# The last block's last three output tiles in two halves of 256 tokens, in a written order, with weights and residuals held in free buffers

## The chip, the cores and the metric

The kernel runs on one core of one Trainium2 chip. The metric is the device time of one execution in microseconds. The core has TensorE (PE in the rows, its weight loads PEld), VectorE (DVE), ScalarE (ACT), GpSimd (POOL), and DMA engines that are fed by the queues of SyncE (SP) and of ACT.

## What is computed

Two layers of a bidirectional encoder trunk over 2048 tokens of 1024 channels, then a final RMSNorm. What matters here is the end of the second layer:

```python
    gate = jax.nn.sigmoid(gate_lg + gate_b).reshape(bsz, seq, N_BRANCH, D_MODEL)
    y = gate[:, :, 0] * y_a + gate[:, :, 1] * y_b
    return y @ w_out
...
        x = x + hybrid_mixer(h, w_in[l], qkv_conv_w[l], a_log[l], dt_bias[l], dn_norm_w[l],
...
    return rms_norm(x, final_norm_w)
```

The product with `w_out` and the residual give x for all 1024 channels of a token; only then is the token's mean square known, and each channel is scaled by its inverse root and by `final_norm_w`.

## The kernel before

Channels lie on the 128 partitions, tokens along the free axis. `merge` of the last layer works on halves of 1024 tokens: for each it makes the gated sum y, split into a high and a low part (`yhi`, `ylo`), and calls `last_out`. `last_out` runs over two blocks of 512 tokens. In a block, j runs over eight output tiles of 128 channels. For each j, `dense` issues 24 matmuls of 512 columns (8 steps over the input channels, three each: high weight by high y, L174, high weight by low y, L175, low weight by high y, L176) into a PSUM bank `pd`; DVE adds the residual `xr` (L1304) into `xl`; ACT squares it (L225) and DVE adds the square to `ss` (L226). After the eighth tile, `token_sum` (L200) sums the squares over the partitions with matmuls of one column, `rsqrt` makes the inverse root with nine short DVE operations, `spread` makes a diagonal `dg` (L206) and spreads it over the partitions with matmuls of 128 columns (L208), and eight DVE operations of 512 columns (L1317) scale the tiles, each followed by the store of its tile (L1320), even j on SP's queue and odd j on ACT's.

The weights of a tile come through `weight`: two transfers of 256 KB each into one of two buffers `wraw`, then a split in ACT (L157, high part `whi`) and in DVE (L158, low part `wlo`). A transfer into a `wraw` buffer waits until DVE has split what lay in it two transfers earlier. `whi` and `wlo` have two buffers each, so weights are made ready one tile ahead. The tiles `xr`, `sq` and `dg` share three buffers. Large buffers come from a pool of four; in the last half two of them hold the gate products' operands (`uop`, `gop`), which nothing reads after the gates of that half, and two hold `yhi` and `ylo`.

Nothing in `last_out` has an order written out: a scheduler places each instruction on its engine's queue, by its estimates of when the operands are there, and within an engine the queue is run in order. SP's queue holds the loads of weights and residuals and half of the stores in one row, so a load that waits holds back all that stand behind it. `bind(start)` fixes the order as written for all instructions issued since `mark()`, on PE, ACT, DVE and POOL; SP is left out of it.

Of the kernel before, what the change touches and what calls it, by code (L numbers as in the profile page):

```python
# [14 lines left out]
P = 128  # L15
L = 2048
HALF = 1024
NB = 512
D = 1024
KD = 8  # L20
# [4 lines left out]
EPS = 1e-6  # L25
# [5 lines left out]
STEP = (4, 4, 4, 4)  # L31
TAIL = (3, 3, 2)
Z = '121'
LATE = 4
AHEAD = 4
R2 = 3.7
# [40 lines left out]
class Trunk:  # L77
# [79 lines left out]
        self.nc.scalar.activation(hi, src, AF.Copy)  # L157
        self.nc.vector.tensor_tensor(out=lo, in0=src, in1=hi.bitcast(F32), op=ALU.subtract)  # L158

    def weight(self, src, kk):  # L160
        hi = self.pw.tile([P, KD, P], F32R, tag="whi", bufs=2, name="whi")[:, 0:kk, :]
        lo = self.pw.tile([P, KD, P], F32R, tag="wlo", bufs=2, name="wlo")[:, 0:kk, :]
# [35 lines left out]
    def token_sum(self, ps, src, n):  # L198
        for i in range(n):
            self.nc.tensor.matmul(ps[:, i:i + 1], src[:, i * P:(i + 1) * P], self.ones[:, 0:1],  # L200
                                  start=True, stop=True)

    def spread(self, ps, r, n):
        dg = self.pst.tile([P, NB], F32, tag="st", name="dg").rearrange("p (a b) -> p a b", b=P)
        for i in range(n):
            self.nc.vector.tensor_scalar(out=dg[:, i, :], in0=self.ident, scalar1=r[:, i:i + 1],  # L206
                                         scalar2=None, op0=ALU.mult)
            self.nc.tensor.matmul(ps[:, i * P:(i + 1) * P], self.ones, dg[:, i, :], start=True, stop=True)  # L208
# [11 lines left out]
    def add_square(self, ss, x, first):  # L220
        if first:
            self.nc.scalar.activation(ss, x, AF.Square)
        else:
            sq = self.st("sq")
# [518 lines left out]
    def conformer_norm(self, blk):  # L743
# [12 lines left out]
        yield 1.8  # L756
        for _ in range(int(Z[0])):
            yield 0.0
# [8 lines left out]
        yield 4.0  # L767
        for _ in range(int(Z[1])):
            yield 0.0
# [6 lines left out]
        yield 1.5  # L776
        for _ in range(int(Z[2])):
            yield 0.0
# [502 lines left out]
    def late_norm(self, xn, ss, wcol):  # L1281
        for _ in range(LATE):
            yield
        r = self.norm_stats(ss)
        yield
        yield
        yield from self.normalise(1, xn, r, wcol)

    def last_out(self, l, half, xd, fnw, yhi, ylo, ahead):
        nc, a = self.nc, self.a  # L1290
        v_ = nc.vector
        for b in range(2):
            sl = slice(b * NB, (b + 1) * NB)
            tk = slice(half * HALF + b * NB, half * HALF + (b + 1) * NB)
            xn = [t[:, i * NB:(i + 1) * NB] for t in (self.mid("xl"), self.mid("xl")) for i in range(4)]
            ss = self.hm("ss")[:, 0:NB]
            w = self.weight(a["w_out"][l, 0], KD)
            for j in range(KD):
                next(ahead, None)
                ps = self.pd()  # L1300
                self.dense(ps, w, lambda k: (yhi[:, k, sl], ylo[:, k, sl]), KD)
                xr = self.st("xr")
                self.load(xr, xd[j][:, tk])
                v_.tensor_tensor(out=cut(xn[j]), in0=sort(ps), in1=cut(xr), op=ALU.add)  # L1304
                self.add_square(ss, xn[j], j == 0)
                if j + 1 < KD:
                    w = self.weight(a["w_out"][l, j + 1], KD)
            ps = self.pz()
            self.token_sum(ps, ss, 4)
            v = self.sm(4, "nv")  # L1310
            r = self.sm(4, "nr")
            v_.tensor_scalar(out=v, in0=ps[:, 0:4], scalar1=1.0 / D, scalar2=EPS, op0=ALU.mult, op1=ALU.add)
            self.rsqrt(r, v, 4)
            pr = self.pz()
            self.spread(pr, r, 4)
            for j in range(KD):
                v_.scalar_tensor_tensor(out=xn[j], in0=xn[j], scalar=fnw[:, j:j + 1], in1=pr,  # L1317
                                        op0=ALU.mult, op1=ALU.mult)
                eng = nc.scalar if j % 2 else nc.sync
                eng.dma_start(a["out"][j, :, tk], xn[j])  # L1320


def layout(inputs, depth):
# [49 lines left out]
```

## Time and profile before

| | |
|---|---|
| median of 3 runs | 3189.29 us (3188.14 to 3192.9) |
| the profiled execution | 3187.47 us |
| its span | 3185.7 us |
| PE busy | 3090.6 us, 97% of the span |
| DVE busy | 2398.4 us, 75% |
| ACT busy | 1385.3 us, 43% |
| mean granted TensorE clock | 0.993 |

The profiled execution is 1.77 us longer than its span and 1.82 us shorter than the median. Times of rows are counted from the start of the span. A busy share over the whole span says little of the last 60 us, in which everything that is changed lies; there the timeline, the chain of work that ended last and the busy time of stretches are read. The granted clock of 1.00 is TensorE's 2.4 GHz, 0.50 its 1.2 GHz.

### The profile page before, as it was taken

The page shows a single profiled execution, that of the slowest core. Times are in us where ns is not written, and L with a number is a line of the kernel's source. Part 1 is how long each engine was busy: PE and PEld are TensorE (multiplying, and loading weights), DVE is VectorE, ACT ScalarE, POOL GpSimd, SP SyncE. Part 2 cuts the span into 40 slices and gives each one's busy share as a digit, 9 for nine tenths or more (in the row PEclk, how much of TensorE's full clock was granted, in tenths as well). Part 3 has the DMA queues.
Part 4 walks back from the last instruction along what each step waited for, and adds up shares of the span by engine and source line. Part 5 has one row for each costly group of instructions (what it writes and reads, how often), then busy time and mean ns, then how long its engine had stood idle before and what let it go on. Part 6 is the DMA issues. An engine that isn't in the chain of part 4 may idle for free. (4 is left out here: it accounts for less than half of the span.)

```text
span 3185.7 us, 51259 instructions
## 1 busy us (share of the span) xinstructions
PE 3090.6 (97%) x19110; PEld 2705.8 (85%) x19110; DVE 2398.4 (75%) x4409; ACT 1385.3 (43%) x3104; POOL 302.3 (9%) x297
## 2 busy tenths in 40 slices
PE   6999999999999999999999999999999999999997
PEld 5788888888889998787888888888888999878786
DVE  7789898987646697745676989898955567867655
ACT  5625151522444466533345242425234445655332
POOL 3000000000122231000000000000002222200000
PEclk9999999999999999999999999999999999999999
DMA  4323222334687886654413131414357777855634
GB/s 141 90 96 93 87 93 87 93 112 133 206 288 247 258 267 208 198 185 133 135 53 101 66 120 60 120 60 123 117 186 261 243 252 255 283 182 192 204 126 146
DMA packets 427545, 501.70 MB, mean 157 GB/s; under 512 B 96224, under 2 KB 260704, under 8 KB 427296
## 3 DMA queue, kind: packets, MB, share of 16 engines
q1 hardware_dynamic: 354544, 388.58, 39.2%
q10 hardware_dynamic: 64688, 80.09, 7.3%
q0 software_dynamic: 8064, 29.76, 2.5%
q8 instruction: 150, 2.46, 0.3%
q14 instruction: 99, 0.81, 0.1%
HBM read 342.74 MB, written 155.58 MB: 156 GB/s over the span
## 5 line engine op out<-in xcount | busy, mean ns | idle before, releaser
L174 PE MATMUL pd<-h,whi 128*128 128x512 f32 x2816 | 1092.1, 388 | 0.0
L176 PE MATMUL pd<-h,wlo 128*128 128x512 f32 x2816 | 1070.4, 380 | 1.9 <-DVE wlo L158 1.9
L175 PE MATMUL pd<-h,whi 128*128 128x512 f32 x2816 | 1070.9, 380 | 0.0
L728 DVE SCALAR_TENSOR_TENSOR cacc<-gp,vec,cacc 128x1009 f32<-128x1009 f32 (+1 forms) x480 | 614.3, 1280 | 37.5 <-ACT cacc L726 34.3
L176 PEld LDWEIGHTS pd<-h,wlo 128*128 128x128 f32 x2816 | 533.8, 190 | 79.3 <-DVE wlo L158 3.5
L174 PEld LDWEIGHTS pd<-h,whi 128*128 128x128 f32 x2816 | 534.0, 190 | 79.0 <-issue 1.4
L175 PEld LDWEIGHTS pd<-h,whi 128*128 128x128 f32 x2816 | 534.5, 190 | 72.4 <-issue 1.9
L157 ACT ACTIVATE whi<-wraw 128x512 fp32r<-128x512 f32 x400 | 242.7, 623 | 473.2 <-PE pd L175 335.9
L158 DVE TENSOR_TENSOR wlo<-wraw,whi 128x512 fp32r<-128x512 f32 x400 | 275.0, 701 | 142.1 <-ACT whi L157 141.8
L553 DVE SCALAR_TENSOR_TENSOR acc<-cin,vec,acc 128x1022 f32<-128x1022 f32 (+1 forms) x192 | 246.5, 1299 | 14.4 <-ACT acc L551 13.2
L176 PE MATMUL pd<-yhi,wlo 128*128 128x512 f32 x512 | 194.9, 381 | 3.8 <-DVE wlo L158 3.7
L174 PE MATMUL pd<-yhi,whi 128*128 128x512 f32 x512 | 194.6, 380 | 0.9 <-ACT whi L157 0.9
L175 PE MATMUL pd<-ylo,whi 128*128 128x512 f32 x512 | 194.0, 379 | 0.0
L808 ACT ACTIVATE go<-pd,vec 128x512 f32<-128x512 f32 x128 | 87.1, 680 | 147.9 <-PE pd L176 138.2
L529 ACT ACTIVATE cin<-pd 128x512 f32<-128x512 f32 x96 | 57.0, 594 | 154.7 <-PE pd L176 154.6
L176 PEld LDWEIGHTS pd<-yhi,wlo 128*128 128x128 f32 x512 | 96.8, 189 | 19.9 <-DVE wlo L158 6.4
L740 ACT ACTIVATE ao<-pd 128x512 f32<-128x512 f32 x64 | 38.3, 598 | 170.0 <-PE pd L176 169.9
L174 PEld LDWEIGHTS pd<-yhi,whi 128*128 128x128 f32 x512 | 96.8, 189 | 15.4 <-ACT whi L157 2.0
L175 PEld LDWEIGHTS pd<-ylo,whi 128*128 128x128 f32 x512 | 96.8, 189 | 13.6
L174 PE MATMUL pd<-uop,whi 128*128 128x512 f32 x256 | 101.0, 395 | 6.6 <-ACT whi L157 6.5
L176 PE MATMUL pd<-uop,wlo 128*128 128x512 f32 x256 | 99.1, 387 | 2.3 <-DVE wlo L158 1.4
L175 PE MATMUL pd<-gop,whi 128*128 128x512 f32 x256 | 97.7, 381 | 3.0 <-DVE gop L158 3.0
(297 smaller groups left out, 4754.9 us busy)
## 6 DMA issues: line engine op xcount, KB each, us to landing
wraw<-w_in SPq DMA_DIRECT2D x240, 256.0 KB, 3.3
gt<-go ACTq DMA_DIRECT2D x128, 256.0 KB, 3.6
dl<-gr SPq DMA_DIRECT2D x128, 256.0 KB, 5.2
dl<-kq SPq DMA_DIRECT2D x64, 512.0 KB, 6.1
dl<-kv SPq DMA_DIRECT2D x64, 512.0 KB, 5.8
wraw<-w_out SPq DMA_DIRECT2D x96, 256.0 KB, 3.0
kq<-acc SPq DMA_DIRECT2D x16, 1024.0 KB, 5.5
gr<-go ACTq DMA_DIRECT2D x64, 256.0 KB, 2.2
```

The source lines that it names most:

```text
L157: self.nc.scalar.activation(hi, src, AF.Copy)
L158: self.nc.vector.tensor_tensor(out=lo, in0=src, in1=hi.bitcast(F32), op=ALU.subtract)
L174: mm(ps, whi[:, k, :], xhi, start=k == 0, stop=False)
L175: mm(ps, whi[:, k, :], xlo, start=False, stop=False)
L176: mm(ps, wlo[:, k, :], xhi, start=False, stop=k == kk - 1)
L529: nc.scalar.activation(cut(t[:, o + b * NB:o + (b + 1) * NB]), sort(ps), AF.Copy)
L553: self.nc.vector.scalar_tensor_tensor(out=out, in0=t[:, k:k + n], scalar=wc(k), in1=out, op0=ALU.mult, op1=ALU.add)
L728: self.nc.vector.scalar_tensor_tensor(out=acc, in0=t[:, k:k + n], scalar=wc(k), in1=acc, op0=ALU.mult, op1=ALU.add)
L740: nc.scalar.activation(cut(o), sort(ps), func)
L808: nc.scalar.activation(cut(o), sort(ps), AF.Identity, bias=self.vec[:, V_GB + j:V_GB + j + 1])
```

## The change

For the last block of the last half, the first five tiles (`PART`) run as before. The weights of tiles 5, 6 and 7 are loaded during tiles 1, 2 and 3 into a free large buffer (`wend`), through the same two `wraw` buffers, and their residuals into another (`xend`). Then the three tiles run first for tokens 0 to 255 of the block and then for tokens 256 to 511, as matmuls of 256 columns, in an order fixed by `bind`. The closing steps (token sum, root, spread, scaling, stores) run once for each half: those of the first half stand among the products of the second. The square of the last tile of a half isn't added to `ss`; a second group of one-column matmuls adds it in PSUM (`token_add`). The lines of `after` are numbered higher, as L146 for the load that was L145, L158 and L159 for the split, L178 to L180 for the three matmuls, L209 and L217 for the sum and the spread, L1307 for the residual's addition, L1331 for the scaling.

```diff
-    def weight(self, src, kk):
+    def weight(self, src, kk, kept=None):
+        if kept:
+            hi, lo = kept
...
+    def token_add(self, ps, src, n, first, last):
+        for i in range(n):
+            self.nc.tensor.matmul(ps[:, i:i + 1], src[:, i * P:(i + 1) * P], self.ones[:, 0:1],
+                                  start=first and i == 0, stop=last, skip_group_check=True)
...
+        def close(o, n, sq):
+            q = n // P
+            c = slice(o % NB, o % NB + n)
+            ps = self.pz()
+            self.token_add(ps, ss[:, c], q, True, sq is None)
+            if sq is not None:
+                self.token_add(ps, sq, q, False, True)
...
+            self.rsqrt(r, v, q)
+            yield
+            pr = self.pz()[:, 0:n]
+            self.spread(pr, r, q)
+            yield
+            for j in range(KD):
+                x = xn[j][:, c]
+                v_.scalar_tensor_tensor(out=x, in0=x, scalar=fnw[:, j:j + 1], in1=pr, op0=ALU.mult, op1=ALU.mult)
+                eng = nc.scalar if j % 2 else nc.sync
+                eng.dma_start(a["out"][j, :, half * HALF + o:half * HALF + o + n], x)
+                yield
...
+            whole = PART if half and b else KD
+            if whole < KD:
+                hold = self.big([P, 2, KD, NB], F32R, "wend").rearrange("p a b c -> p (a b c)")
+                parts = [hold[:, i * D:(i + 1) * D].rearrange("p (k c) -> p k c", c=P) for i in range(2 * (KD - whole))]
+                ws = []
+                spare = self.big([P, 8192], F32, "xend")
+                late = [spare[:, i * NB:(i + 1) * NB] for i in range(KD - whole)]
...
+                if j + 1 < whole:
                     w = self.weight(a["w_out"][l, j + 1], KD)
...
+                if whole < KD and j and len(ws) < KD - whole:
+                    i = len(ws)
+                    ws.append(self.weight(a["w_out"][l, whole + i], KD, parts[2 * i:2 * i + 2]))
+                    self.load(late[i], xd[whole + i][:, half * HALF + o:half * HALF + o + NB])
...
+            start = self.mark()
+            n = NB // 2
+            first = iter(())
+            for h in range(2):
+                g = o + h * n
+                for i, (j, w) in enumerate(zip(range(whole, KD), ws)):
+                    p = product(j, w, g, n, late[i][:, h * n:h * n + n])
+                    if h and i == 1:
+                        run(first, 1)
+                    if h and i == 2:
+                        run(p, 3)
+                        run(first, 1)
+                        run(p, 5)
+                        run(first, 4)
+                    run(p)
+                    x = xn[j][:, h * n:h * n + n]
+                    if j + 1 < KD:
+                        self.add_square(ss[:, h * n:h * n + n], x, False)
+                sq = self.st("sq")[:, 0:n]
+                nc.scalar.activation(sq, x, AF.Square)
+                c = close(g, n, sq)
+                if h == 0:
+                    first = c
+                else:
+                    run(first, 2)
+                    run(c, 1)
+                    run(first)
+                    run(c)
+            self.bind(start)
```

Up to the third tile of the last block (j = 2) the order on every engine is the same as before. Three places differ in what the prediction needs. The first is SP's queue from the residual of j = 2 on. Before, the weights of j = 3 stand there (`wraw_27828`, `wraw_27832`), then those of j = 4 (`wraw_27869`, `wraw_27873`) and of j = 5:

```order
L145 DMA xr_27820<-x1_11761 128x512
L145 DMA wraw_27828<-w_out 128x512
L145 DMA wraw_27832<-w_out 128x512
L145 DMA wraw_27869<-w_out 128x512
L145 DMA wraw_27873<-w_out 128x512
L145 DMA xr_27861<-x1_11761 128x512
L145 DMA wraw_27910<-w_out 128x512
L145 DMA wraw_27914<-w_out 128x512
```

Now `wraw_27797` and `wraw_27801` are the weights of j = 5, which are kept, `wraw_27839` and `wraw_27843` those of j = 3, `wraw_27847` and `wraw_27851` those of j = 6, `wraw_27889` and `wraw_27893` those of j = 4:

```order
L146 DMA xr_27806<-x1_11761 128x512
L146 DMA wraw_27797<-w_out 128x512
L146 DMA wraw_27801<-w_out 128x512
L146 DMA xend_27706<-x1_11761 128x512 x2
L146 DMA wraw_27839<-w_out 128x512
L146 DMA wraw_27843<-w_out 128x512
L146 DMA xr_27856<-x1_11761 128x512
L146 DMA xend_27706<-x1_11761 128x512
L146 DMA wraw_27847<-w_out 128x512
L146 DMA wraw_27851<-w_out 128x512
L146 DMA wraw_27889<-w_out 128x512
L146 DMA wraw_27893<-w_out 128x512
```

So two transfers of kept weights and two residuals stand ahead of the weights of j = 3, and two more with a third residual ahead of those of j = 4.

The second place is ACT around the square of j = 3. Before, the square (`sq_27864`) stands behind the splits for j = 4 (`whi_27867`) and j = 5 (`whi_27908`):

```order
L157 ACTIVATE whi_27867<-wraw_27869 128x512
L157 ACTIVATE whi_27867<-wraw_27873 128x512
L157 ACTIVATE whi_27908<-wraw_27910 128x512
L157 ACTIVATE whi_27908<-wraw_27914 128x512
L225 ACTIVATE sq_27864<-xl_27702 128x512
```

Now the square of j = 3 (`sq_27884`) stands ahead of the split for j = 4 (`whi_27887`), behind that for j = 6:

```order
L158 ACTIVATE wend_27705<-wraw_27847 128x512
L158 ACTIVATE wend_27705<-wraw_27851 128x512
L234 ACTIVATE sq_27884<-xl_27702 128x512
L158 ACTIVATE whi_27887<-wraw_27889 128x512
L158 ACTIVATE whi_27887<-wraw_27893 128x512
```

The split for j = 4 has moved behind an operation that needs the product of j = 3.

The third place is the end of DVE's queue. Before, the root (its last step is L196) is followed by the diagonal and eight scalings of 512 columns:

```order
L195 TENSOR_TENSOR rst_28039<-rst_28039,nr_28037 128x4
L196 SCALAR_TENSOR_TENSOR nr_28037<-rst_28039,nr_28037 128x4
L206 TENSOR_SCALAR dg_28053<-con_90,nr_28037 128x128 x4
L1317 SCALAR_TENSOR_TENSOR xl_27702<-xl_27702,fnw_96,pz_28052 128x512 x4
L1317 SCALAR_TENSOR_TENSOR xl_27703<-xl_27703,fnw_96,pz_28052 128x512 x4
```

Now, behind the second half's root, the last two scalings of the first half (with `pz_28112`) come first:

```order
L200 SCALAR_TENSOR_TENSOR nr_28154<-rst_28156,nr_28154 128x2
L1331 SCALAR_TENSOR_TENSOR xl_27703<-xl_27703,fnw_96,pz_28112 128x256 x2
L215 TENSOR_SCALAR dg_28174<-con_90,nr_28154 128x128 x2
L1331 SCALAR_TENSOR_TENSOR xl_27702<-xl_27702,fnw_96,pz_28173 128x256 x4
L1331 SCALAR_TENSOR_TENSOR xl_27703<-xl_27703,fnw_96,pz_28173 128x256 x4
```

So ten scalings of 256 columns stand behind the last root instead of eight of 512. On PE, the first half's token sum stands behind the first product of the second half, and its spread behind nine matmuls of that half's third product.

## Rows read from the trace of the kernel before

**Rows 1.** The timeline (start, length, engine, line, operation, count), PE alone, from the last matmul of the last product on.

```profile
3166.97 0.38 PE L176 MATMUL pd<-yhi,wlo 128*128 128x512 f32 x1
3169.58 1.55 PE L200 MATMUL pz<-con,ss 128*128 128x1 f32 x8 [2.22 <-DVE ss L226]
3173.74 2.08 PE L208 MATMUL pz<-dg,con 128*128 128x128 f32 x8 [2.62 <-DVE dg L206]
```

**Rows 2.** The timeline, DVE alone, over the last two products and the closing steps.

```profile
3162.21 0.69 DVE L1304 TENSOR_TENSOR xl<-pd,xr 128x512 f32<-128x512 f32 x1 [1.43 <-PE pd L176]
...
3167.39 0.69 DVE L1304 TENSOR_TENSOR xl<-pd,xr 128x512 f32<-128x512 f32 x1 [3.04 <-PE pd L176]
3168.83 0.69 DVE L226 TENSOR_TENSOR ss<-ss,sq 128x512 f32<-128x512 f32 x1 [0.74 <-ACT sq L225]
3171.16 0.16 DVE L1312 TENSOR_SCALAR nv<-pz 128x4 f32<-128x4 f32 x1 [1.64 <-PE pz L200]
...
3173.40 0.87 DVE L206 TENSOR_SCALAR dg<-con,nr 128x128 f32<-128x128 f32 x4
3175.86 5.36 DVE L1317 SCALAR_TENSOR_TENSOR xl<-xl,fnw,pz 128x512 f32<-128x512 f32 x8 [1.58 <-PE pz L208]
```

**Rows 3.** The chain of work that ended last, in order of time (start, length, what), from the weights of j = 3 to the first low-part matmul of j = 4.

```profile
3135.03 4.15 DMA wraw<-w_out
...
3139.28 0.64 ACT whi L157
...
3139.95 0.70 DVE wlo L158
3140.66 4.62 DMA wraw<-w_out
...
3145.39 0.64 ACT whi L157
3146.07 0.48 PE pd L174
...
3146.80 0.48 PE pd L176
```

**Rows 4.** The timeline, PE alone: the first low-part matmul of j = 2, its last matmul and the first of j = 3.

```profile
3135.05 0.48 PE L176 MATMUL pd<-yhi,wlo 128*128 128x512 f32 x1 [1.42 <-DVE wlo L158]
...
3139.69 0.38 PE L176 MATMUL pd<-yhi,wlo 128*128 128x512 f32 x1
3139.97 0.48 PE L174 MATMUL pd<-yhi,whi 128*128 128x512 f32 x1
```

**Rows 5.** The tile `wraw` from 3120 us on: time from the issue of a transfer to its landing.

```profile
DMA to landing us min/median/max: 2.4/2.9/4.7
```

**Rows 6.** The timeline, PE alone: the previous block's token sum (eight one-column matmuls), the first matmul behind it, and that block's spread.

```profile
3122.97 1.05 PE L200 MATMUL pz<-con,ss 128*128 128x1 f32 x8
3123.89 0.46 PE L174 MATMUL pd<-yhi,whi 128*128 128x512 f32 x1
...
3126.65 1.16 PE L208 MATMUL pz<-dg,con 128*128 128x128 f32 x8
```

**Rows 7.** The timeline, PE alone, in the delta rule's stage: sixteen matmuls of 128 columns and what follows them.

```profile
1241.44 1.95 PE L983 MATMUL pz<-dl,dl 128*128 128x128 f32 x16
1243.32 0.23 PE L924 MATMUL pz<-dh,dh 32*32 32x32 f32 x4
```

**Rows 8.** Groups of weight loads by line and form (count, busy us, mean ns of one, idle time before).

```profile
L176 PEld LDWEIGHTS pd<-yhi,wlo 128*128 128x128 f32 x512 | 96.8, 189 | 19.9 <-DVE wlo L158 6.4
...
L983 PEld LDWEIGHTS pz<-dl,dl 128*128 128x128 f32 x512 | 62.2, 192 | 1.7
```

**Rows 9.** The same view of DVE: operations of 128, 512 and 256 columns.

```profile
L972 DVE SCALAR_TENSOR_TENSOR dl<-pz,neg,dl 128x128 f32<-128x128 f32 x240 | 66.4, 343 | 17.8 <-PE pz L967 17.1
...
L1317 DVE SCALAR_TENSOR_TENSOR xl<-xl,fnw,pz 128x512 f32<-128x512 f32 x32 | 21.4, 743 | 3.0 <-PE pz L208 2.9
...
L694 DVE TENSOR_TENSOR sol<-sol,solt 128x256 f32<-128x256 f32 x8 | 3.4, 421 | 0.2
```

**Rows 10.** The same view of ACT: operations of 128 and 512 columns.

```profile
L976 ACT ACTIVATE dm<-pz,eg 128x128 f32<-128x128 f32 x240 | 68.6, 368 | 56.6 <-PE pz L970 56.6
...
L225 ACT ACTIVATE sq<-xl 128x512 f32<-128x512 f32 x28 | 17.4, 622 | 13.1 <-DVE xl L1304 9.8 <-issue 3.0 <-DMA gt<-gt 0.2
```

**Rows 11.** Busy time of each engine in stretches (length, then PE, PEld, DVE, ACT, POOL busy with counts, then granted clock, DMA share, GB/s): around two idle times of PE earlier in the program.

```profile
1230.70:1234.60 3.90, 0.00 (x0) 0.00 (x0) 1.77 (x3) 3.87 (x9) 0.00 (x0) 1.00 0.56 192
1234.60:1238.00 3.40, 3.08 (x14) 3.08 (x15) 3.35 (x10) 0.44 (x2) 1.26 (x1) 0.50 0.73 218
1238.00:1241.00 3.00, 3.00 (x46) 2.58 (x45) 2.86 (x11) 2.35 (x7) 1.25 (x1) 1.00 0.84 223
...
1447.80:1449.90 2.10, 0.06 (x1) 0.00 (x0) 0.52 (x1) 2.10 (x4) 0.00 (x0) 1.00 0.00 0
1449.90:1453.00 3.10, 2.96 (x13) 2.29 (x13) 2.58 (x5) 0.98 (x2) 0.00 (x0) 1.00 0.52 75
```

**Rows 12.** The same view of the end: the last four products, and what comes behind them.

```profile
3146.00:3167.40 21.40, 21.25 (x96) 17.98 (x96) 10.53 (x17) 6.57 (x12) 0.00 (x0) 1.00 0.38 123
3167.40:3185.70 18.30, 3.62 (x16) 3.24 (x16) 9.47 (x26) 0.63 (x1) 0.00 (x0) 0.57 0.31 115
```

More of the change, by code (lines that the diff above doesn't have):

```diff
@@ L33 @@
 Z = '121'
+PART = 5
 LATE = 4
@@ L158, in split @@
         self.nc.vector.tensor_tensor(out=lo, in0=src, in1=hi.bitcast(F32), op=ALU.subtract)
-    def weight(self, src, kk):
-        hi = self.pw.tile([P, KD, P], F32R, tag="whi", bufs=2, name="whi")[:, 0:kk, :]
-        lo = self.pw.tile([P, KD, P], F32R, tag="wlo", bufs=2, name="wlo")[:, 0:kk, :]
+    def weight(self, src, kk, kept=None):
+        if kept:
+            hi, lo = kept
+        else:
+            hi = self.pw.tile([P, KD, P], F32R, tag="whi", bufs=2, name="whi")[:, 0:kk, :]
+            lo = self.pw.tile([P, KD, P], F32R, tag="wlo", bufs=2, name="wlo")[:, 0:kk, :]
         for k in range(0, kk, 4):
@@ L223, in add_square @@
         else:
-            sq = self.st("sq")
+            sq = self.st("sq")[:, 0:x.shape[1]]
             self.nc.scalar.activation(sq, x, AF.Square)
@@ L1291, in last_out, with product, residual @@
         v_ = nc.vector
+        def product(j, w, o, n, xr):
+            sl = slice(o, o + n)
+            ps = self.pd()[:, 0:n]
+            yield from self.dense_steps(ps, w, lambda k: (yhi[:, k, sl], ylo[:, k, sl]), KD)
+            x = xn[j][:, o % NB:o % NB + n]
+            v_.tensor_tensor(out=cut(x), in0=sort(ps), in1=cut(xr), op=ALU.add)
+        def residual(j, o, n):
+            xr = self.st("xr")[:, 0:n]
+            self.load(xr, xd[j][:, half * HALF + o:half * HALF + o + n])
+            return xr
@@ new lines, in close @@
+        def close(o, n, sq):
[5 more added lines that the diff above has]
+                self.token_add(ps, sq, q, False, True)
+            v = self.sm(q, "nv")
+            r = self.sm(q, "nr")
+            v_.tensor_scalar(out=v, in0=ps[:, 0:q], scalar1=1.0 / D, scalar2=EPS, op0=ALU.mult, op1=ALU.add)
+            self.rsqrt(r, v, q)
[9 more added lines that the diff above has]
+                yield
@@ L1292, in last_out, with run @@
+        def run(g, n=1000):
+            for _ in range(n):
+                if next(g, self) is self:
+                    return
         for b in range(2):
-            sl = slice(b * NB, (b + 1) * NB)
-            tk = slice(half * HALF + b * NB, half * HALF + (b + 1) * NB)
+            o = b * NB
             xn = [t[:, i * NB:(i + 1) * NB] for t in (self.mid("xl"), self.mid("xl")) for i in range(4)]
             ss = self.hm("ss")[:, 0:NB]
+            whole = PART if half and b else KD
[5 more added lines that the diff above has]
+                late = [spare[:, i * NB:(i + 1) * NB] for i in range(KD - whole)]
@@ L1297, in last_out @@
             w = self.weight(a["w_out"][l, 0], KD)
-            for j in range(KD):
+            for j in range(whole):
                 next(ahead, None)
[L1300 to L1304, printed above, removed]
+                run(product(j, w, o, NB, residual(j, o, NB)))
+                if self.rate:
+                    self.follow()
@@ L1305, in last_out @@
                 self.add_square(ss, xn[j], j == 0)
-                if j + 1 < KD:
+                if j + 1 < whole:
                     w = self.weight(a["w_out"][l, j + 1], KD)
[L1308 to L1320, printed above, removed]
+                if whole < KD and j and len(ws) < KD - whole:
+                    i = len(ws)
+                    ws.append(self.weight(a["w_out"][l, whole + i], KD, parts[2 * i:2 * i + 2]))
+                    self.load(late[i], xd[whole + i][:, half * HALF + o:half * HALF + o + NB])
@@ new lines, in last_out @@
+            if whole == KD:
+                run(close(o, NB, None))
+                continue
+            start = self.mark()
[21 more added lines that the diff above has]
+                    first = c
+                else:
+                    run(first, 2)
+                    run(c, 1)
+                    run(first)
+                    run(c)
```

## The prediction

> **What bounds the kernel now.** I read the stretches first: in the last four products PE is busy 21.25 of 21.40 us, behind them 3.62 of 18.30 us, and DVE 9.47 [rows 12]. So PE bounds the program up to its last product, and behind it a chain. The timelines of PE and DVE show the chain [rows 1, 2]: the last matmul is issued at 3166.97, DVE takes its bank at 3167.39 (0.42 later), then residual, square, `ss`, token sum, root from 3171.16, diagonal at 3173.40, spread, eight scalings from 3175.86 to 3181.22, stores, end at 3185.7. That is 18.3 us in which nothing overlaps. Half of the tokens could go through these steps under the other half's products, which is the part that the change takes up.
>
> The third view is the chain of waits ahead of it [rows 3]. The two transfers of j = 3 are issued at 3135.03, the first takes 4.15 us, its split 0.64 in ACT and 0.70 in DVE, and only then, at 3140.66, does a buffer come free for j = 4's first: a turn of 5.63 us, while a product takes 5.18 (3162.21 to 3167.39 [rows 2]). The stretch is supplied barely in time: j = 3 starts 0.28 us after the last matmul of j = 2 is issued (3139.69, 3139.97 [rows 4]), j = 4 waits for its weights [rows 3]. The change puts more loads into just this stretch.
>
> **Supply: j = 3.** In SP's queue the kept weights of j = 5 now stand where those of j = 3 stood; both pass through the same two `wraw` buffers, so j = 3's weights get the turn that j = 4 had, issued at 3140.66 [rows 3]. Their landing takes 2.4 to 4.7 us [rows 5]; the same turn took 4.62 with a residual behind it [rows 3]; I take 3.4, between the median of 2.9 and that. With 0.11 to the start of ACT, 0.64 of split and 0.04, PE starts j = 3 at 3144.8 instead of 3139.97 (3143.8 at 2.4, 3146.1 at 4.62). Nothing else stands ahead in PE's queue, so the 4.8 us are idle.
>
> **Supply: j = 4.** Call the start of j = 3 S. Two bounds follow. By the loads: the split of j = 3's first piece ends at S + 0.7, then come j = 6's first piece (2.9 + 0.1 + 0.64 + 0.70) and j = 4's (2.9 + 0.1 + 0.64 + 0.05): S + 8.7. By ACT's order: the square of j = 3 now stands ahead of the split of j = 4's weights, so that product has to end first. Its first low-part matmul comes 0.73 after its first (as at 3146.07 and 3146.80 [rows 3]) instead of 0.43, so S + 0.3 + 5.18 + 0.2 for the product to reach DVE, 0.69 for the residual, 0.1, 0.64 for the square, 0.64 for the split: S + 7.8. I take S + 8.7. Then j = 4 lasts 5.18 and 0.35 more for three matmuls of tile 5 that the scheduler put between its first and its third, which cover the wait for the low part. PE is past j = 4 at S + 14.2.
>
> **The narrow products.** 72 matmuls of 512 columns (0.216 each, 5.18 / 24) become 144 of 256. The trace has none of 256 in this form. From below: half of 0.216 is 0.108. From above: 0.216, as if width didn't matter. The nearest rows are those that the weight load paces: eight one-column matmuls in 0.92 us, 0.115 each [rows 6], sixteen of 128 columns in 1.88, 0.118 each [rows 7], and the loads last alike in both kinds, 189 and 192 ns [rows 8]. I take 0.115: 141 behind j = 4 make 16.2 us.
>
> The Trainium skill ("TensorE: Matmul & The Clock Gate", "The mechanism") says that a weight load overlaps a running matmul only where the two use other row groups. Here all 128 rows are used, so by it each load would stand beside its matmul. The rows speak against it: 0.216 for 512 columns at 2.4 GHz is 0.213 of streaming, so loads of 128 columns are hidden there. What it would give is the second rival.
>
> **Work put between the products.** The first half's token sum, eight passes, 0.9 [rows 6]; its spread, four of the eight passes of [rows 6], 0.45; and a wait ahead of that spread: DVE makes the diagonal behind tile 6's residual, square and `ss` (0.2 + 0.42 + 0.5 + 0.42 + 0.3), while only nine matmuls (1.0) stand between: 0.8. The last matmul then reaches DVE 0.2 us after the pace. So DVE gets the last bank at S + 14.2 + 16.2 + 0.9 + 0.45 + 0.8 + 0.2 = S + 32.75 = 3177.55, instead of 3167.39: **10.2 us later**. Of these, 4.8 come ahead of S, 3.5 from the wait for j = 4 (8.7 - 5.18), 1.0 from the narrow matmuls (16.55 for 15.5) and 2.2 from the closing steps, less 1.5 of waits that the old stretch held (3139.97 to 3167.39 is 27.4 us, five products are 25.9).
>
> **The end.** A DVE operation of 256 columns lasts 0.42 [rows 9] against 0.69 [rows 2]. ACT's square, between 0.368 at 128 and 0.622 at 512 columns [rows 10], is 0.45. Scaling: 743 - 343 ns for 384 columns [rows 9] makes 0.476 for 256, and in a row 0.40 each (5.36 for eight of 512 is 0.66 each). The chain: residual 0.42, square 0.45, no `ss`, two hand-overs 0.1, four passes of the sum 0.6 (1.05 for eight at full clock [rows 6]), root 2.24 as before (3171.16 to 3173.40 [rows 2]), two scalings of the first half that stand ahead of the diagonal 0.8, diagonal to PE 0.35, four passes of the spread 0.9 (half of 1.16 [rows 6] to half of 2.08 [rows 1], the clock being 0.57 there [rows 12]), eight scalings 3.3, and 4.48 from the last scaling to the end as before (3181.22 to 3185.7). Sum 13.65 against 18.3: **4.65 us less**. The first half's scalings and stores lie under tile 7's last matmuls; without that cover they would add 3.3.
>
> **Sum.** 10.2 - 4.65 = +5.5 us on the profiled execution's 3187.47: 3193.0. The median lies 1.82 above that execution, so 3189.29 + 5.5 = **3194.8 us**. A measurement of this kernel tells 0.2%, 6.4 us, from no change; the forecast is just inside. Bounds of the case: with landings at 2.4 us, j = 4 goes by ACT's order (S + 7.8) and S is 1.0 earlier, and 0.5 less wait at the spread: 3192.4. With 4.62 at j = 3 and at one of the next two, 3.0 more: 3197.8. The 4.8 us of idle also touch the clock: after PE's idle time up to 1234.6 the granted clock is 0.50 for the next 3.4 us, after 2.1 us at 1447.8 it stays 1.00 [rows 11]. If it falls, j = 3 loses up to 1.7 us, of which the 0.9 between the two bounds for j = 4 hides a part: 0.8 more.
>
> **Rivals.**
> First, the clock and the loads together: the clock falls in the wait for j = 3, a late landing delays j = 4 by 1.7, and the second idle time (from the end of j = 3 to j = 4, about 3 us, between the two) lets it fall again, so that j = 4 and the first narrow matmuls run at 0.50 for some 3.4 us (1.7 lost). 3194.8 + 1.7 + 0.8 + 1.7 = 3199 us, 0.3% **slower**. It decides if that second idle time is followed by the lower clock, as the one of 3.9 us was and the one of 2.1 wasn't. For it: both idle times are new; against: the loads' median.
>
> Second, weight loads beside the narrow matmuls: 0.115 + 0.108 instead of 0.115, 144 times: +15.5 us, 3210, slower. It decides from 0.13 per matmul on (2.1 us more). Against it: [rows 6, 7] and the hidden loads of the wide ones. This is what the page's rule named above would do.
>
> Third, the loads are hidden after all (j = 3 and j = 4 start as before, since the extra transfers fill gaps): then 1.05 + 0.9 + 0.45 + 0.8 = 3.2 less 4.65 are left, 3188 us, no difference; even with the old waits of 1.5 gone as well it is 3186, and the whole gain at the end, 4.65, is under 6.4. Against it: the kept loads can't fill a gap, because they hold the two buffers for which the next weights wait.
>
> **Chances.** Forecast 0.66, and its upper part above 6.4 us is a third of it: 0.44 within 0.2%, 0.22 slower. First rival 0.20, of which 0.04 within. Second 0.05, slower. Third 0.09: 0.06 within, 0.03 faster. Together faster 0.03, within 0.54, slower 0.43. The range leaves out the third and the second rival: 3190.5 (the forecast's lower bound with 1.8 for the spread of the median) to 3200 (the first rival and 1).
>
> **What would show it.** Right: PE idle for 4 to 6 us between j = 2 and j = 3 with ACT's split as releaser, 2 to 4 us ahead of j = 4, matmuls of 256 columns 0.11 to 0.12 us apart, 13 to 14 us from the last residual addition to the end, the clock at 0.50 once in j = 3. Wrong: j = 3 within 2 us of its old start, or narrow matmuls over 0.13 us apart. The turn of the two buffers is the step that I lean on most.

## The result, and the profile after

| | |
|---|---|
| before, measured beside it | 3192.9 us median of 15 runs |
| after | 3199.79 us median of 15 runs (3190.34 to 3210.14) |
| ratio | 1.0024, 95% interval 1.0014 to 1.0033 |
| profiled execution after | 3199.07 us, span 3197.3 us |

The kernel became slower by 0.24%, just over the 0.2% that the prediction took as its bound; the interval also holds values under it. On the 3189.29 us from which the forecast was reckoned the ratio makes 7.7 us; the forecast was 5.5.

The two traces can't be laid upon each other from the start: j = 2's first low-part matmul stands at 3135.05 before [rows 4] and at 3139.38 after, though nothing ahead of it has changed. So every kernel below is measured from its residual addition of j = 1 in the last block (3138.04 after), in three stretches: to the residual addition of j = 4, from there to the last residual addition, and from there to the end. The rows are busy times of the engines in these stretches; the first number behind the bounds is the length, the last three are granted clock, DMA share and GB/s. Before:

```profile
3133.72:3152.03 18.31, 16.56 (x72) 13.37 (x73) 8.86 (x15) 6.07 (x10) 0.00 (x0) 1.00 0.51 158
3152.03:3167.39 15.36, 15.32 (x71) 13.07 (x70) 6.73 (x11) 4.20 (x7) 0.00 (x0) 1.00 0.37 117
3167.39:3185.68 18.29, 3.62 (x16) 3.24 (x16) 9.48 (x26) 0.63 (x1) 0.00 (x0) 0.57 0.31 115
```

The same three of after, and then the clock from the idle time before j = 3 to j = 4:

```profile
3138.04:3166.28 28.24, 19.39 (x75) 15.94 (x76) 11.95 (x19) 8.71 (x14) 0.00 (x0) 0.88 0.55 166
3166.28:3184.30 18.02, 17.34 (x156) 17.15 (x154) 9.02 (x29) 2.71 (x6) 0.00 (x0) 1.00 0.02 6
3184.30:3197.30 13.00, 2.13 (x11) 1.67 (x10) 7.45 (x27) 0.42 (x1) 0.00 (x0) 0.60 0.46 155
...
3144.40:3149.35 4.95, 0.00 (x0) 0.00 (x0) 2.63 (x4) 1.98 (x4) 0.00 (x0) 1.00 0.43 140
3149.35:3152.75 3.40, 2.81 (x7) 2.22 (x8) 1.39 (x2) 1.17 (x2) 0.00 (x0) 0.50 0.68 218
3152.75:3156.77 4.02, 4.02 (x19) 3.19 (x17) 1.35 (x2) 1.26 (x2) 0.00 (x0) 1.00 0.36 123
3156.77:3159.59 2.82, 0.86 (x5) 0.81 (x6) 2.02 (x4) 1.15 (x2) 0.00 (x0) 1.00 0.65 179
3159.59:3162.99 3.40, 3.40 (x10) 2.77 (x9) 0.89 (x2) 1.26 (x2) 0.00 (x0) 0.50 0.56 178
```

The whole is 59.26 us instead of 51.96: **+7.3**. The first stretch is 9.93 longer; the second, with the narrow products and the closing steps of the first half, 2.66 longer; the end 5.29 shorter. So the last two stretches gain 2.6 us and the first, with the supply, costs 9.9. The clock fell to 0.50 twice for 3.4 us, once from just ahead of j = 3 and once 0.86 us into j = 4.

The chain of waits of after answers to [rows 3]:

```profile
3139.35 5.82 DMA wraw<-w_out
3145.19 0.64 ACT wend L158
3145.85 0.70 DVE wend L159
3146.57 2.60 DMA wraw<-w_out
3149.26 0.64 ACT whi L158
3149.94 0.80 PE pd L178
3150.74 0.43 PE pd L179
...
3156.80 0.70 DVE xl L1307
3157.53 0.20 ACT sq L234
3157.73 0.34 issue
3158.07 0.62 ACT whi L158
3158.73 0.48 PE pd L178
```

It is read link by link: the kept weights of j = 5 land, ACT and DVE split them (`wend`), only then are j = 3's weights issued, land and are split (`whi`), and PE starts. Matmuls then stand 0.43 us apart, twice the usual 0.216. The start of j = 4 hangs on ACT: the square of j = 3 and right behind it the split. PE's timeline answers to [rows 1, 4]:

```profile
3144.01 0.38 PE L180 MATMUL pd<-yhi,wlo 128*128 128x512 f32 x1
3149.94 0.80 PE L178 MATMUL pd<-yhi,whi 128*128 128x512 f32 x1 [5.55 <-ACT whi L158]
...
3158.73 0.48 PE L178 MATMUL pd<-yhi,whi 128*128 128x512 f32 x1 [1.97 <-ACT whi L158]
...
3159.60 0.71 PE L180 MATMUL pd<-yhi,wlo 128*128 128x512 f32 x1
...
3166.08 0.27 PE L178 MATMUL pd<-yhi,wend 128*128 128x256 f32 x1
...
3169.99 0.28 PE L180 MATMUL pd<-yhi,wend 128*128 128x256 f32 x1
...
3181.88 0.71 PE L217 MATMUL pz<-dg,con 128*128 128x128 f32 x4 [0.68 <-DVE dg L215]
3185.29 0.61 PE L209 MATMUL pz<-con,sq 128*128 128x1 f32 x4 [0.68 <-ACT sq L1387]
3189.17 1.22 PE L217 MATMUL pz<-dg,con 128*128 128x128 f32 x4 [3.27 <-DVE dg L215]
```

The idle times are 5.55 and 1.97 us. The row at 3159.60 is the first low-part matmul of j = 4; the scheduler put three narrow matmuls of tile 5 ahead of it. From 3166.08 to 3169.99 there are 35 steps of a narrow matmul, 0.112 us each. The weight loads by form say how long one load is, the 48 of one of the three lines (answers to [rows 8]):

```profile
L180 PEld LDWEIGHTS pd<-yhi,wend 128*128 128x128 f32 x48 | 9.2, 192 | 0.0
```

A load's record lasts 192 ns, as before, and still a matmul starts every 112 ns: the records of the loads overlap one another as well (the 154 of the second stretch would make 29.6 us end to end and fill 17.15). DVE's timeline shows the end (answers to [rows 2]), and the tile `wraw` its landings (answers to [rows 5]):

```profile
3184.30 0.42 DVE L1307 TENSOR_TENSOR xl<-pd,xend 128x256 f32<-128x256 f32 x1
...
3188.05 0.87 DVE L1331 SCALAR_TENSOR_TENSOR xl<-xl,fnw,pz 128x256 f32<-128x256 f32 x2
3190.43 3.22 DVE L1331 SCALAR_TENSOR_TENSOR xl<-xl,fnw,pz 128x256 f32<-128x256 f32 x8 [1.12 <-PE pz L217]
...
DMA to landing us min/median/max: 2.5/2.8/5.9
```

The last scaling ends at 3193.65, the span 3.65 later; before it was 4.48.

### The profile page after: what moved, and what is told of

It reads as the page before. It is cut to its first block, busy times and chain, and to the rows that moved or that the text cites. A ratio compares the mean times of both kernels' runs of the same rounds, so it can differ in the third digit from the quotient of the medians.

```text
span 3197.3 us, 51459 instructions
## 1 busy us (share of the span) xinstructions
PE 3097.9 (97%) x19190; PEld 2716.4 (85%) x19190; DVE 2403.0 (75%) x4433; ACT 1385.2 (43%) x3107; POOL 300.8 (9%) x297
## 5 line engine op out<-in xcount | busy, mean ns | idle before, releaser
L178 PE MATMUL pd<-h,whi 128*128 128x512 f32 x2816 | 1093.3, 388 | 0.0
L180 PE MATMUL pd<-h,wlo 128*128 128x512 f32 x2816 | 1072.6, 381 | 2.1 <-DVE wlo L159 2.1
L178 PEld LDWEIGHTS pd<-h,whi 128*128 128x128 f32 x2816 | 535.2, 190 | 78.8 <-issue 1.4
L180 PEld LDWEIGHTS pd<-h,wlo 128*128 128x128 f32 x2816 | 534.9, 190 | 78.9 <-DVE wlo L159 3.7
L158 ACT ACTIVATE whi<-wraw 128x512 fp32r<-128x512 f32 x394 | 239.1, 623 | 465.0 <-PE pd L179 349.1
L159 DVE TENSOR_TENSOR wlo<-wraw,whi 128x512 fp32r<-128x512 f32 x394 | 272.8, 706 | 129.0 <-ACT whi L158 128.4
L178 PE MATMUL pd<-yhi,whi 128*128 128x512 f32 x488 | 186.9, 383 | 8.0 <-ACT whi L158 8.0
L180 PE MATMUL pd<-yhi,wlo 128*128 128x512 f32 x488 | 187.0, 383 | 3.4 <-DVE wlo L159 3.4
L179 PE MATMUL pd<-ylo,whi 128*128 128x512 f32 x488 | 186.1, 381 | 0.0
L178 PEld LDWEIGHTS pd<-yhi,whi 128*128 128x128 f32 x488 | 93.2, 191 | 22.1 <-ACT whi L158 9.2
L178 PE MATMUL pd<-uop,whi 128*128 128x512 f32 x256 | 102.3, 400 | 7.8 <-ACT whi L158 7.7
L180 PEld LDWEIGHTS pd<-yhi,wlo 128*128 128x128 f32 x488 | 92.9, 190 | 18.2 <-DVE wlo L159 5.2
L180 PE MATMUL pd<-uop,wlo 128*128 128x512 f32 x256 | 100.4, 392 | 2.1 <-DVE wlo L159 1.4
```

What stands on the lines that cost most here:

```text
L178: mm(ps, whi[:, k, :], xhi, start=k == 0, stop=False)
L179: mm(ps, whi[:, k, :], xlo, start=False, stop=False)
L180: mm(ps, wlo[:, k, :], xhi, start=False, stop=k == kk - 1)
```

## The experiments

My theory: the halves gain as predicted, and all of the loss is the place of the kept loads ahead of j = 3's and j = 4's in the two `wraw` buffers, with the clock's fall as its second part. The rivals: the loads would be hidden and the narrow products or the closing steps cost more than the rows show; or the clock alone is the loss. The table has each kernel's time, its ratio to the kernel before on the same chip, and its three stretches in us.

| kernel | us | ratio, 95% interval | to j = 4 | to the last addition | to the end | sum |
|---|---|---|---|---|---|---|
| before | | | 18.31 | 15.36 | 18.29 | 51.96 |
| after | 3199.79 | 1.0024, 1.0014 to 1.0033 | 28.24 | 18.02 | 13.00 | 59.26 |
| kept weights last | 3193.34 | 0.9997, 0.9987 to 1.0006 | 20.93 | 17.37 | 13.00 | 51.30 |
| own staging | 3188.49 | 0.9983, 0.9974 to 0.9991 | 18.33 | 18.36 | 12.99 | 49.68 |
| kept, whole width | 3202.65 | 1.0026, 1.0015 to 1.0038 | 26.94 | 15.11 | 17.35 | 59.40 |
| filler matmuls | 3198.56 | 1.0017, 1.0008 to 1.0026 | 25.70 | 18.31 | 12.99 | 57.00 |
| own staging, whole width | 3196.70 | 1.0001, 0.9993 to 1.0010 | 18.51 | 15.54 | 17.59 | 51.64 |
| own staging, one closing | 3194.34 | 0.9999, 0.9990 to 1.0008 | 18.11 | 16.08 | 16.15 | 50.34 |
| own staging, reordered | 3192.23 | 0.9989, 0.9980 to 0.9999 | 16.99 | 17.70 | 12.34 | 47.03 |
| own staging, again | 3189.97 | 0.9993, 0.9984 to 1.0002 | 16.81 | 18.36 | 12.85 | 48.02 |
| reordered, again | 3189.35 | 0.9989, 0.9980 to 0.9998 | 17.16 | 17.69 | 12.29 | 47.14 |

The kernel before had 3193.82 us beside the first four experiments, 3195.1 beside the next three and 3192.68 beside the last two, so ratios are compared, not times. The stretches come from one trace of each kernel.

**Kept weights last.** The kept tiles are loaded during tiles 3 and 4, behind the regular weights; all else is as in the change.

```diff
-                if whole < KD and j and len(ws) < KD - whole:
+                for _ in range(min(j - 2, 2) if whole < KD and j > 2 else 0):
```

> The kept weights of tiles 5, 6 and 7 are loaded behind the regular ones (order 3, 4, 5, 6, 7 in place of 5, 3, 6, 4, 7), all else as in the changed kernel. Load-order theory (the time is lost because j = 3 and j = 4 wait for weights that stand behind kept ones): j = 3 and j = 4 start as in the kernel before, tiles 6 and 7 may wait some 2.5 us, the narrow products and the first half's closing steps cost 3.2 us and the end gives 5.3 back: 0 to +1 us against the kernel before, ratio 0.9995 to 1.0005. Rival (the narrow products and the closing steps between them cost more than the end gives back, whatever the order of loads): still about +7 us, 1.002.

As the load-order theory expected, the loss was gone: the sum is 51.30 us, and the first stretch fell from 28.24 to 20.93 (it is still longer than before because DVE takes j = 4's bank late, at 3154.67, when PE has begun tile 6). The clock stayed at 1.00 up to the end. The first transfer of j = 3's weights landed after 3.98 us, and PE waits a little for the kept weights of tiles 6 and 7, 1.6 us in four waits, where some 2.5 had been expected (a row of the chain of waits and the longest wait in PE's timeline):

```profile
3135.05 3.98 DMA wraw<-w_out
...
3154.09 0.38 PE L178 MATMUL pd<-yhi,wend 128*128 128x256 f32 x1 [0.67 <-ACT wend L158]
```

So the order of the loads alone decides between slower and no difference. The two buffers are still the limit; the wait has only moved to where it is shorter.

**Own staging.** The kept weights land in six buffers of their own, in free parts of `xend`, and no longer pass through `wraw`. The scheduler now issues them in the block before.

```diff
-                raw = self.pw.tile([P, 4, P], F32, tag="wraw", bufs=2, name="wraw")
+                if raws:
+                    raw = raws[k // 4]
+                else:
+                    raw = self.pw.tile([P, 4, P], F32, tag="wraw", bufs=2, name="wraw")
...
+                raws = [spare[:, (4 + i) * NB:(5 + i) * NB].rearrange("p (k c) -> p k c", c=P) for i in range(2 * (KD - whole))]
```

> The kept weights land in six buffers of their own in the free large buffer instead of the two shared staging buffers; nothing else is edited, and with nothing to wait for the scheduler puts their transfers and splits into the block before, one tile's worth around each of its first three tiles. Load-order theory: no idle time ahead of j = 3 and j = 4 beyond that of the kernel before (0.3 and 1.0 us), no fall of the clock there, narrow products and closing steps +3.2, end -5.3: 2 to 4 us under the kernel before, ratio 0.9988 to 0.9995. Rival (narrow products and closing steps): about +7 us, 1.002.

Its stretches:

```profile
3140.21:3158.54 18.33, 16.41 (x72) 13.21 (x73) 7.66 (x14) 4.90 (x8) 0.00 (x0) 1.00 0.43 128
3158.54:3176.90 18.36, 17.68 (x159) 17.49 (x157) 9.02 (x30) 2.71 (x6) 0.00 (x0) 1.00 0.02 7
3176.90:3189.89 12.99, 2.13 (x11) 1.67 (x10) 7.44 (x27) 0.42 (x1) 0.00 (x0) 0.69 0.46 154
```

The first is as long as before (18.31), the other two as in after but for 0.34 in the second: the three narrow matmuls that after had put into j = 4. With the supply out of the way the halves show their gain, 2.28 us in all. The early loads lie outside of these stretches, in the block before, and cost nothing there: from the first matmul of the last half's products to the residual addition of j = 1 it is 54.93 us here as in the kernel before. The time lay lower than this stretch explains (0.9983 where 2.28 us are 0.9993), so it was measured a second time, below.

**Kept, whole width.** The change's loads, but tiles 5 to 7 run at 512 columns with one closing, as before.

```diff
-            for h in range(2):
...
+            for i in range(KD - whole):
+                run(product(whole + i, ws[i], o, NB, late[i]))
+                self.add_square(ss, xn[whole + i], False)
+            run(close(o, NB, None))
```

> The loads of the changed kernel, in its order, but tiles 5, 6 and 7 run at the full width of 512 tokens, and one closing runs at the end as in the kernel before. Load-order theory: j = 3 and j = 4 wait as in the changed kernel and the clock falls, while the end is the old one of 18.3 us: +9 to +10 us against the kernel before, ratio 1.003. Rival (narrow products and closing steps): both are gone, so within 2 us of the kernel before, 1.000.

Without any halves the loss stays, so narrow matmuls and closing steps aren't the cause. It is +7.44 us where 9 to 10 were expected: no fall of the clock came in j = 4 (5.92 us from its first matmul to its residual addition, 7.55 in after), and the end was 0.94 shorter than before with the same instructions. Its clock, from the idle time before j = 3 to j = 4:

```profile
3142.33:3145.39 3.06, 0.00 (x0) 0.00 (x0) 1.95 (x3) 1.59 (x3) 0.00 (x0) 1.00 0.39 133
3145.39:3152.19 6.80, 5.13 (x12) 4.08 (x13) 2.67 (x4) 2.19 (x4) 0.00 (x0) 0.50 0.66 208
3152.19:3155.04 2.85, 2.85 (x13) 2.15 (x12) 0.79 (x2) 0.63 (x1) 0.00 (x0) 1.00 0.31 97
3155.04:3157.00 1.96, 0.00 (x0) 0.00 (x0) 1.23 (x2) 1.20 (x3) 0.00 (x0) 1.00 0.85 258
3157.00:3163.00 6.00, 6.00 (x28) 5.25 (x29) 2.73 (x6) 1.70 (x3) 0.00 (x0) 1.00 0.27 89
```

Here one fall of 6.8 us covers most of j = 3, and the same idle time of 1.96 us ahead of j = 4 is followed by none. PE's timeline has the start of j = 3:

```profile
3147.06 0.80 PE L178 MATMUL pd<-yhi,whi 128*128 128x512 f32 x1 [4.74 <-ACT whi L158]
```

j = 4 starts at 3157.00, 9.94 us later, against 8.79 in after. In both, ACT goes from the square of j = 3 straight to j = 4's split without waiting for the landing, so here the longer fall held j = 4 back through ACT's order.

**Filler matmuls.** The change, with 16 and 8 matmuls of 512 columns into a bank that nothing reads, ahead of j = 3 and j = 4, chained to their place on PE. The loads are in the order of the change; on ACT the scheduler put the split of j = 4's first piece ahead of the square of j = 3.

```diff
+FILL = {3: 16, 4: 8}
...
+                for k in range(FILL[j]):
+                    self.nc.tensor.matmul(pf, yhi[:, k % KD, 0:P], mix(yhi[:, k % KD, sl]), start=True, stop=True)
```

> The changed kernel with 16 more matmuls of 512 columns ahead of j = 3 and 8 ahead of j = 4, whose result nothing reads; they run while PE waits for weights (5.6 and 2.0 us idle in the changed kernel). If the lower clock behind the two idle times is part of the cost (0.43 instead of 0.216 us for some 6 and 8 matmuls): the clock stays at 1.00 in j = 3 and j = 4 and the time is 2 to 3 us under the changed kernel, ratio to the kernel before 1.0015. If only the waits themselves cost: no change against the changed kernel, 1.0024, or up to 1 us more where a wait is shorter than the filling.

The clock stayed at 1.00 up to the end's chain. The first stretch, and the chain of waits:

```profile
3141.30:3167.00 25.70, 21.71 (x97) 17.80 (x98) 11.77 (x19) 8.71 (x14) 0.00 (x0) 1.00 0.60 183
...
3142.61 5.05 DMA wraw<-w_out
...
3157.66 2.72 DMA wraw<-w_out
3160.49 0.64 ACT whi L167
3161.17 0.48 PE pd L187
...
3161.90 0.48 PE pd L189
```

The sum is 2.26 us under after, within the 2 to 3 that the theory of the clock expected; the times alone don't show it, as the intervals of the two ratios overlap. j = 4 itself is 1.72 shorter (its first matmul to its residual addition is 5.83, 3161.17 to 3167.00, against 7.55, 3158.73 to 3166.28), the first landing 0.77 (5.05 against 5.82), which the fillers don't explain, and the second stretch is 0.29 longer, since the three narrow matmuls are back in it. From the first low-part matmul on, where both kernels do the same, j = 4 takes 5.10 (from 3161.90) against 6.68 (from 3159.60): the fall in j = 4 cost 1.58 us.

The fall in j = 3 cost little. Here j = 3 (from 3152.44) ran at full clock, and j = 4 still started 8.73 us behind it, held by its weights, whose landing took 2.72 us. In after that landing took 2.5, so the loads alone would have let j = 4 start about 8.5 behind j = 3; it started at 8.79, held by ACT's order, which the half clock had made late. That is at most 0.3 us, worked out from one trace of each.

**Own staging, whole width.** Early loads with their own buffers, and no halves (the diffs of the two kernels above, together).

> The weights of tiles 5 to 7 land early in buffers of their own (as in the run with its own staging buffers), but the three tiles run at whole width with one closing, as in the kernel before. This is the price of the loads alone, without the halves. My theory: that run's gain of about 2.3 us on its stretch (residual addition of j = 1 to the end) has two parts, a supply that no longer waits (the old stretch held about 1.5 us of waits, and none would be left: -1 to -2 us) and the halves (about 3.2 us of narrow products and closing steps against 5.3 us less behind the last residual addition: about -1 to -2 us). So this kernel comes out 1 to 2 us under the kernel before, ratio 0.9994 to 0.9998, with no idle of PE between j = 2 and j = 7 over 0.6 us. Rival A: the gain was all in the early loads, and the halves are worth nothing: 0.9983. Rival B: it was all in the halves: 1.0000.

A miss: no gain of 1 to 2 us, but 0.3, and the ratio is 1.0001. PE's timeline says why:

```profile
3140.27 0.48 PE L183 MATMUL pd<-yhi,wlo 128*128 128x512 f32 x1 [1.41 <-DVE wlo L159]
3151.67 0.48 PE L181 MATMUL pd<-yhi,whi 128*128 128x512 f32 x1 [0.51 <-ACT whi L158]
...
3175.18 1.05 PE L212 MATMUL pz<-con,ss 128*128 128x1 f32 x8 [2.23 <-DVE ss L238]
```

The wait for j = 2's low part, 1.42 before [rows 4], is still there, since these weights don't change their way, and so is one ahead of j = 4. Those two waits aren't made by the weights that were taken away. Rival B fits: early loads alone are worth nothing that can be measured, and the gain of own staging is the halves': its last two stretches are 31.35 us (18.36 and 12.99) against 33.13 here.

**Own staging, one closing.** Narrow products in the written order, and a single closing of 512 tokens at the end.

```diff
-                c = close(g, n, sq)
...
+            run(close(o, NB, None))
```

> Own staging buffers, the three tiles in two halves of 256 tokens in the written order, but a single closing at whole width behind the last product. It has the narrow products without the closing steps in between. By the profile of the changed kernel, narrow matmuls stand 0.11 us apart, 144 of them 15.9 us against 15.5 us for 72 wide ones: my theory expects 0.3 to 0.6 us more than the kernel with early loads and whole width (plus up to 0.4 us less, since the last residual addition and square are 256 columns wide). Rival (weight loads beside narrow matmuls cost more than the pace shows): more than 2 us above that kernel.

The second stretch is 0.54 us longer than at whole width, as expected: this is the price of narrow matmuls. The end is 1.44 shorter, where up to 0.4 was expected. PE's timeline:

```profile
3173.75 0.50 PE L212 MATMUL pz<-con,ss 128*128 128x1 f32 x4
3175.40 0.61 PE L212 MATMUL pz<-con,ss 128*128 128x1 f32 x4 [1.14 <-DVE ss L238]
```

Four passes of the token sum are done before the last addition to `ss`, and behind it (residual, square and addition on 256 columns) PE waited 1.14 us for the other four; at whole width it waited 2.23 for all eight (the last row of the fence before). Then the closing steps between the products cost 2.28 more (16.08 to 18.36) and give back 3.16 (16.15 to 12.99).

**Own staging, reordered.** Tile 4's weights are kept too; the first half's spread stands behind fifteen matmuls of the last product instead of nine; three of the first half's scalings stand behind the second half's diagonal.

```diff
+                if whole < KD and j + 2 == whole:
+                    w = ws[0]
...
                     if h and i == 2:
-                        run(p, 3)
-                        run(first, 1)
                         run(p, 5)
-                        run(first, 4)
+                        run(first, 1)
+                        run(p, 3)
+                        run(first, 2)
...
-                    run(first, 2)
-                    run(c, 1)
+                    run(first, 3)
+                    run(c, 2)
```

> The run with own staging buffers, and three places in its order mended: tile 4's weights are kept too (no wait ahead of j = 4, 0.5 us), the first half's spread stands behind fifteen matmuls of the last product instead of nine (PE waited 0.68 us for the diagonal), and six of the first half's eight scalings are placed so that the second half's diagonal comes out no later than two operations behind its root, with the last ones behind the second half's spread (0.8 us). My theory: each wait is on the path, so it comes out 1.5 to 2 us under the run with own staging buffers, ratio 0.9976 to 0.9980 to the kernel before. Rival: what is saved ahead of the diagonal comes back behind it, because DVE's scalings and the stores end the program in any case: 0.9983, as that run.

The second stretch lost 0.66 us, as much as the wait ahead of the spread (0.68), and the end 0.65 (0.8 expected). The ratio of 0.9989 is a miss: 0.9976 to 0.9980 was expected, reckoned from own staging's 0.9983.

**The two best, again.** The kernel with own staging and the reordered one, unchanged, on one chip.

> The same kernel as the one with own staging buffers, timed beside the reordered one on one chip. Its stretch from the residual addition of j = 1 to the end was 2.3 us shorter than in the kernel before, which is a ratio of 0.9993; its time gave 0.9983 with 0.9974 to 0.9991. My theory: the stretch tells the truth and the time lay low by chance, so 0.9990 to 0.9995 now. Rival: something outside of the last block gained too, 0.9983 again.

> The same kernel as the reordered one. Its stretch was 47.03 us, 2.65 less than that of the kernel with own staging buffers and 4.93 less than before, a ratio of 0.9985; its time gave 0.9989 with 0.9980 to 0.9999. My theory: 0.9983 to 0.9988 now, and 2 to 3 us under the other kernel of this call. Rival: the two are alike in time, and the difference in the stretch is lost elsewhere.

Own staging came out at 0.9993, as its traced stretch had said, so the 0.9983 held some chance; but its first part was 16.81 us this time instead of 18.33, with the same instructions. That part varies by 1.5 us with the landings, and the parts behind it by 0.14. For the reordered kernel both expectations missed: 0.9989 is above 0.9988, and the medians differ by 0.6 us and not by 2 to 3.

Reordering is worth 1.2 to 1.3 us behind j = 4 (30.04 and 29.98 against 31.35 and 31.21), but the rival of its second expectation is right in part, for some is lost ahead of the stretches. From the first matmul of the last half's products to the residual addition of j = 1 it is 54.93 and 54.94 us in the two traces of own staging, 55.17 and 55.84 in the two of the reordered kernel, which brings two more pieces of weights through ACT and DVE there. In the second of them PE waited once for a split:

```profile
3097.86 0.48 PE L181 MATMUL pd<-yhi,whi 128*128 128x512 f32 x1 [0.34 <-ACT whi L158]
```

With that part, the two repeated kernels are alike (102.96 and 102.98 us to the end), and the intervals of their times overlap. So it isn't shown that reordering is faster than own staging. Against the kernel before the reordered one is faster in both measurements, by 0.1%.

## Why the prediction failed where it did

The mechanism was right: kept loads hold the two buffers, PE waits, and the end's gain is smaller than the wait. The size was wrong: the forecast was inside 0.2%, the result outside, and a second fall of the clock, which only the first rival had (with 0.20), made most of the difference. Term by term, on the stretch:

| step of the prediction | taken | measured |
|---|---|---|
| start of j = 3, later by (10.56 us behind j = 2's first low-part matmul, before 4.92) | 4.8 | 5.64 |
| j = 4 behind j = 3 | 8.7 | 8.79 |
| j = 4's start to DVE's taking its bank | 5.7 | 7.55 |
| from there to the last bank, closing steps included | 18.35 | 18.02 |
| the end | -4.65 | -5.29 |
| sum | +5.5 | +7.3 |

**The step that failed** is the clock's place in "Sum". The forecast lets j = 4 run at full clock ("Then j = 4 lasts 5.18 and 0.35 more") and says of the clock only "If it falls, j = 3 loses up to 1.7 us ... 0.8 more", outside the sum. Yet it had two idle times of its own, 4.8 us and about 3 (8.7 less 5.7), and of the two in [rows 11] the one of 3.9 us was followed by 0.50, the one of 2.1 was not. The first lay above 3.9, so one fall belonged in the sum; the second lay between, and the sum took it as none. What the runs showed in its place: j = 4 took 7.55 us instead of 5.7, of which the fall cost 1.58 (filler matmuls), while the fall in j = 3 cost at most 0.3. With the 1.58 the forecast would have been 7.1. The place of the price matters: j = 3 was followed by a wait that the loads made in any case, j = 4 by nothing that was late.

**The second term** is the landing. I took j = 3's turn as issued at 3140.66, so the first transfer's 4.15 us [rows 3] unchanged, and the second at 3.4. They were 5.82 and 2.60: +1.67 and -0.8. Behind the first pair of transfers two residuals had been put in the queue, each landing as late as 6 us (DMA share 0.90 from 3138.0 to 3144.4), which I had counted as holders of a place but not as traffic. The runs bear that out: the first transfer at this place took 5.82, 5.05 and 5.05 us in the three kernels with these residuals behind it (after, kept at whole width, filler matmuls), and 3.76 to 4.76 in the eight traces without, the kernel before among them. How much of the 1.67 they made is open, as either group varies by 0.8 to 1.0.

**What held.** The narrow pace was 0.112 (taken 0.115), the wait ahead of the spread 0.68 (taken 0.8). The start of j = 4 behind j = 3 was 8.79 (taken 8.7), but in part by luck: the forecast let the loads bind there and put ACT's order at 7.8, and what came last was ACT's order, because at half clock j = 3's last matmul started 6.45 us behind its first, 5.36 with filler matmuls. The end was 0.64 shorter than taken: 0.83 of that is the carried-over 4.48 from last scaling to end, where the last store has half the bytes now, and the spread took 0.36 back (1.26, 3189.17 to 3190.43, for the 0.9 taken). Of the signs, the clock fell twice and not once, and the second idle time was 1.97, just short of 2 to 4.

**Rivals.** The first, clock and loads together, was right in the place of the second fall and in its price (1.7, measured 1.58), but not by its reason: it expected a fall because an idle time of 3 us would lie between the two of [rows 11], and it measured 1.97, under the 2.1 that no fall had followed. That it fell was luck for this rival. Its 3199 also held 0.8 for j = 3 and 1.7 for a late landing ahead of j = 4; at most 0.3 of the first came, and the landing was late ahead of j = 3 instead, by 0.84. The second, weight loads beside the narrow matmuls, fell: half of a wide matmul's 0.216 us is 0.108, which leaves 4 of the 112 ns for a load. The Trainium skill ("TensorE: Matmul & The Clock Gate", "The mechanism") lets a load overlap a running matmul only where the row groups differ, though the same section also has loads into a background weight buffer pulled ahead; with all 128 rows in use in both, this trace contradicts the first of these, and the measurement decides. The third, loads hidden, fell with kept weights last: where the loads stand decides over 7 us.

## What to carry to other kernels

A prefetch through a staging buffer that the running loop also uses took the loop's turn here, and j = 3 came 5.6 us late. With a landing place of its own, or behind the loop's own loads, the same prefetch cost nothing that could be measured. And where a forecast contains a new idle time of PE, put the clock's price into the sum with a chance, at the place behind which nothing else is late, and not into the bounds alone.

## What the hardware showed that I had not expected

An idle time of 1.97 us ahead of j = 4 was followed by the granted clock of 0.50 in after, and one of 1.96 us in the kernel with kept loads at whole width was not; 2.1 us earlier in the program [rows 11] was not either. Near 2 us the length of an idle time doesn't tell alone; the two kernels differ in what came ahead of it, 4.02 us at full clock behind 3.4 at half in the one, 2.85 behind 6.8 in the other. What decides was not settled. Behind the 1.34 and 1.26 us that were left with filler matmuls it stayed at 1.00.

The last fall lies in the end in each kernel, and its start varies: before at 3169.96, 2.57 us behind the last residual addition, in own staging at whole width at 3177.38, 4.39 behind it, and the same eight one-column matmuls took 1.55 us in the one [rows 1] and 1.05 in the other. At whole width the end took 18.29 us before, 17.59 with own staging and 17.35 with kept loads, so 0.7 to 0.9 us of it come and go without a change of its instructions. Reckoned from the two shorter ends, the halves' gain there is 4.4 to 4.6 us and not 5.29.
